# Head pairs of an RWKV-7 unit in lock-step: small matmuls as unbroken runs, low-rank weights of 128 rows

## The chip, the cores and the metric

The kernel runs on one core of a Trainium2 chip. Five engines work at the same time, each through its own instructions in order: TensorE (PE, matmuls; PEld is its weight loading), VectorE (DVE), ScalarE (ACT), GpSimd (POOL) and SyncE (SP, which here only issues DMAs). The metric is the time of one execution in microseconds; less is better.

## The reference

Two layers of a decoder trunk over 512 tokens of width 1024, in float32. Each layer is a half-step SwiGLU FFN, a mixer and another half-step FFN. The mixer of layer 0 is RWKV-7 time mixing, that of layer 1 a convolution module. The change is in the time mixing:

```python
w = -jax.nn.softplus(-(w0 + jnp.tanh(xw @ w1) @ w2)) - 0.5
a = jax.nn.sigmoid(a0 + (xa @ a1) @ a2)
...
def step(S, inp):
    r_t, w_t, k_t, v_t, a_t, b_t = inp
    sa = jnp.einsum('bhij,bhj->bhi', S, a_t)
    S = (S * w_t[:, :, None, :] + sa[..., None] * b_t[:, :, None, :]
         + v_t[..., None] * k_t[:, :, None, :])
    y_t = jnp.einsum('bhij,bhj->bhi', S, r_t)
    return S, y_t
```

There are 16 heads of size 64. w1, w2, a1 and a2 are low-rank: 1024 to 64 and 64 to 1024.

## The kernel before

Activations lie with the model dimension on the 128 partitions, in 8 blocks, and the 512 tokens along the free dimension. The large products (FFNs, projections) are made of float32 values split into two float32r parts, so each block product is three matmuls of a 128x128 weight against 256 or 512 columns ("wide" below). Weights come in tiles of eight 128x128 blocks (wr), which ACT rounds (wh) and DVE takes the rest of (wl).

The recurrence is done in chunks of 64 tokens. The work is cut into 8 units: unit u holds the head pairs 2q and 2q+1 (q = u mod 4) over one half of the tokens, the first half for units 0 to 3 and the second for units 4 to 7, so four chunks for each of its two pairs. Chunks 0 to 3 in the code are those of the first pair, 4 to 7 those of the second. `unit` has two parts. Part `a` makes the decays, the scaled keys (ka, bkc, bkh), the products G within each chunk, and inverts a triangular matrix block by block (DVE for 16x16 blocks, then matmuls X and D at two levels) into tt. Part `b` runs through the chunks. For each chunk and pair it makes z (PE, from the state in MV), copies it out of PSUM, multiplies by tt (PE), copies the result into UV, multiplies by bk (PE), and updates the state for the next chunk: the old state times the chunk's decay pc plus the product, one DVE instruction for each head. The last chunk's state goes to `carry`, which unit u + 4 starts from. Then y is made (PE), normalised over each head by a chain of small DVE instructions (gm, rq, ra, gr), and gated.

Matmuls differ in their form: 128 rows by 128 columns for the wide ones, 64 by 64 (G, X, D, z times tt, the second part of y), 128 by 64 (z from MV, the product with bk, the first part of y, tv), and 64 by 128 for the second low-rank factors: `step_w2` and the start of `unit` use the upper or lower 64 rows of blocks that hold w2 above a2. The two heads of a pair, h = 0 and 1, write different halves of the PSUM partitions. A small float32 product shows as two records in the trace.

The order of the program is set ahead of time. Every call on an engine goes to the class `Sched` (all of them then show as line 661), which lists the operations with their dependences and places them one by one, with a table of prices (`price`), a price for changing the form on PE (`SWITCH`), and a rule that looks for an operation of the same form first. Before the change nothing keeps the products of one group together. `hold` and `then` keep chains of small DVE instructions in one piece. Where the planner expects PE to stand still for long, it puts matmuls "warm" there, which read a constant and whose result nobody reads.

Of the kernel before, what the change touches and what calls it, by code (L numbers as in the profile page):

```python
# [18 lines left out]
P = 128  # L19
# [205 lines left out]
class Sched:  # L225
# [14 lines left out]
    SWITCH = 0.095  # L240
# [4 lines left out]
    def __init__(self, tc):  # L245
        self.tc = tc
        self.nc = tc.nc
        self.ops = []
        self.extra = []
        self.lead, self.chain, self.last = 0.0, 0, {}  # L250
        self.warmer, self.warm0 = None, 0
        self.hist = {}
        self.cap = {}
# [15 lines left out]
    @staticmethod  # L269
    def box(ap):  # L270
        dims = [tuple(d) for d in ap.ap]
        off = ap.offset
        name = ap.tensor.name
        if ap.space == bass.MemoryType.DRAM:
            return name, 0, 1, off, off + sum((n - 1) * s for s, n in dims) + 1
        ps, pn = dims[0]
        p0 = off // ps if ps else 0
        f0 = off - p0 * ps
        if ap.space == bass.MemoryType.PSUM:
            return name, p0, p0 + pn, 0, T  # L280
        return name, p0, p0 + pn, f0, f0 + sum((n - 1) * s for s, n in dims[1:]) + 1

# [4 lines left out]
    def add(self, engs, meth, args, kw):  # L287
# [57 lines left out]
        self.ops.append(op)  # L345

# [11 lines left out]
    def price(self, e, meth, args, kw, aps, n):  # L358
# [3 lines left out]
        if e == "tensor":  # L362
# [9 lines left out]
            return (0.053 if m > 32 else 0.027) if p0 else max(0.109, n * 1.69e-3)  # L372
# [33 lines left out]
    def order(self):  # L406
# [96 lines left out]
        while front < total:  # L503
            best = None
            for e, h in ready.items():
                if e == "bulk":
                    continue
                tmp, cand, n = [], None, 0
                while h and n < LOOK:
# [40 lines left out]
            if e == "tensor" and not op.bulk and st <= clock[e] + 0.3:  # L550
# [121 lines left out]
class Net:  # L672
# [485 lines left out]
    def unit(self, p):  # L1158
# [141 lines left out]
        for b in LEVELS:  # L1300
            ps = self.psum(f"X{p}_{b}")
            for c in range(NC):
                sl = slice(c * CH, c * CH + CH)
                self.pair(ps[:, sl], G(gb, c, 0), src[:, sl], True, True)
            vec.tensor_tensor(c3(xs), c3(ps), bc(self.c(f"m{b}")), ALU.mult)
            ps = self.psum(f"D{p}_{b}")
            for c in range(NC):
# [3 lines left out]
                else:  # L1311
                    self.pair(ps[:, sl], xs[:, sl], tt[:, sl], True, True)
            if b < 32:
# [15 lines left out]
        ps = self.psum(f"tv{p}")  # L1329
        for c in range(NC):  # L1330
            sl = slice(c * CH, c * CH + CH)
            for h in range(2):
                mm(ps[oth[h], sl], v[:, sl], self.c(f"cen{h}"), start=True, stop=True)
        MV, UV = [S(f"mv{h}") for h in range(2)], [S(f"uv{h}") for h in range(2)]
# [21 lines left out]
        for ci in range(NC):  # L1356
            cc, i = divmod(ci, 2)
            c = i * (NC // 2) + cc
            last = cc == NC // 2 - 1
            sl = slice(c * CH, c * CH + CH)  # L1360
            nx = slice(c * CH + CH, c * CH + 2 * CH)
            pz = self.s.tile(self.ps, [P, T], F32, f"z{p}_{c}", "z", 2)
            z = self.s.tile(self.ms, [P, CH], F32, f"z{p}_{c}", "zs", 4)
            for h in range(2):
                mm(pz[own[h], 0:CH], KA(h, c)[:, :CH], MV[h][:, sl], start=True, stop=True)
            (nc.copier.copy if ZC else vec.tensor_copy)(z, pz[:, 0:CH])
            self.pair(pz[:, CH:2 * CH], tt[:, sl], z, True, True)
            for h, e in ((0, nc.copier if UC else nc.vector), (1, nc.copier if UC else nc.scalar)):
                o = own[h]
                (e.tensor_copy if h == 0 and not UC else e.copy)(UV[h][o, sl], pz[o, CH:2 * CH])  # L1370
            if last and hf:
                continue
            for h in range(2):
                mm(pz[own[h], 2 * CH:3 * CH], bk[c // 4][:, c % 4, h], UV[h][:, sl], start=True, stop=True)
            for h in range(2):
                o = own[h]
                d = self.carry[o, prs[i] * CH:prs[i] * CH + CH] if last else MV[h][o, nx]
                vec.scalar_tensor_tensor(d, MV[h][o, sl], pc[o, c:c + 1],
                                         pz[o, 2 * CH:3 * CH], ALU.mult, ALU.add)
        py = self.psum(f"y{p}")  # L1380
        self.s.after("tensor", UV[1][own[1], YW * CH:YW * CH + CH], 2)
        for c in range(NC):
            sl = slice(c * CH, c * CH + CH)
            for h in range(2):
                mm(py[own[h], sl], MV[h][:, sl], KA(h, c)[:, CH:], start=c == 0, stop=False,
                   skip_group_check=True)
        for c in range(NC):
            sl = slice(c * CH, c * CH + CH)
            for h in range(2):
                o = own[h]  # L1390
                mm(py[o, sl], UV[h][o, sl], G(gb, c, 1)[o], start=False, stop=c == NC - 1,
                   skip_group_check=True)

# [229 lines left out]
class Weights:  # L1623


    def __init__(self, i):
# [10 lines left out]
        self.w2 = blocks(np.concatenate([i["rwkv_w2"][0], i["rwkv_a2"][0]], 0))  # L1637
# [3 lines left out]
    def of(self, kind, *a):  # L1641
# [16 lines left out]
        if kind in ("a", "b"):  # L1658
            q = a[0] % (NB // 2)
            s = self.w2 if kind == "a" else self.g2  # L1660
# [80 lines left out]
```

## Time and profile before

| | |
|---|---|
| median of 3 runs | 2221.14 us (2214.95 to 2223.2) |
| time of the profiled execution | 2214.0 us |
| its span, first to last instruction | 2212.2 us |
| PE busy | 2166.0 us, 98% |
| DVE busy | 1308.6 us, 59% |
| ACT busy | 862.1 us, 39% |
| POOL busy | 514.1 us, 23% |
| mean granted PE clock | 0.995 of full speed |

An engine's busy time is the union of its instructions' spans. The shares are means over stages with different work. The time mixing with its projections lies between about 400 and 960 us of the span.

### The profile page before, as it was taken

What the parts mean: (1) busy time and instruction counts of PE and PEld (TensorE: products, weight loads), DVE (VectorE), ACT (ScalarE), POOL (GpSimd) and SP (SyncE); (2) the same over time, 40 slices, a digit from 0 to 9 for tenths busy, and PEclk for the clock granted to TensorE, in tenths of its full rate; (3) what the DMA queues carried; (4) which work ended last, traced back from release to release, by engine and by line L of the source; (5) the groups of instructions that cost most, each with busy time, mean ns of one, the idle gap of its engine ahead of it and who ended that gap; (6) DMA issues with size and microseconds to landing.
All of it is one profiled execution on the core that took longest, in us unless ns stands there. A gap on an engine that the chain in (4) does not pass through costs nothing.

```text
span 2212.2 us, 38080 instructions
## 1 busy us (share of the span) xinstructions
PE 2166.0 (98%) x15523; PEld 1869.9 (85%) x15523; DVE 1308.6 (59%) x2201; ACT 862.1 (39%) x1374; POOL 514.1 (23%) x488
## 2 busy tenths in 40 slices
PE   9999999899999999999999999999999999999998
PEld 7888889577777888899999888888877799988898
DVE  5333347878788779576443434334469987744454
ACT  4222235555643454454322322122331266532343
POOL 2110113462443143022011112112220142311100
PEclk9999999999999999999999999999999999999999
DMA  4333337123224243356423333333335645543465
GB/s 160 96 95 105 96 105 208 55 78 88 71 71 136 68 122 108 88 179 188 137 93 96 95 94 97 95 95 95 95 108 148 179 137 182 182 132 93 129 189 154
DMA packets 120464, 262.21 MB, mean 119 GB/s; under 512 B 47072, under 2 KB 59744, under 8 KB 120288
## 3 DMA queue, kind: packets, MB, share of 16 engines
q1 hardware_dynamic: 86624, 254.52, 37.8%
q10 hardware_dynamic: 33664, 5.25, 1.3%
q8 instruction: 122, 2.00, 0.4%
q14 instruction: 54, 0.44, 0.1%
HBM read 250.19 MB, written 9.54 MB: 117 GB/s over the span
## 4 chain that ended last, share of the span: by engine, by line
PE 68%; DVE 6%; issue 1%; POOL 1%; ACT 1%; DMA 0%; ACTq 0%; DVEq 0%; POOLq 0%
PE f1d L661 6%; PE f3d L661 6%; PE f3g L661 6%; PE f3u L661 6%; PE f2g L661 6%; PE f2u L661 6%; PE f2d L661 6%; PE f1g L661 5%; PE f1u L661 5%; PE co L661 2%; PE wo L661 2%; PE cg L661 2%; PE ca L661 2%; PE dwx L661 2%; DVE wl L661 1%; PE v L661 1%
## 5 line engine op out<-in xcount | busy, mean ns | idle before, releaser
L661 ACT CAST wh<-wr 128x1024 fp32r<-128x1024 f32 (+1 forms) x448 | 467.4, 1045 | 1017.3 <-issue 376.2
L661 DVE TENSOR_TENSOR wl<-wr,wh 128x1024 fp32r<-128x1024 f32 (+1 forms) x448 | 554.9, 1240 | 263.0 <-ACT wh L661 249.3
L661 POOL TENSOR_TENSOR f0ss<-f0ss,n0rs 128x512 f32<-128x512 f32 x22 | 39.4, 1791 | 255.5 <-ACT f0ss L661 255.5
L661 POOL TENSOR_TENSOR f2ss<-f2ss,n2rs 128x512 f32<-128x512 f32 x22 | 38.8, 1762 | 250.3 <-ACT f2ss L661 250.3
L661 POOL TENSOR_TENSOR f3ss<-f3ss,n3rs 128x256 f32<-128x256 f32 (+1 forms) x33 | 49.6, 1505 | 193.0 <-ACT f3ss L661 193.0
L661 POOL TENSOR_TENSOR f1ss<-f1ss,n1rs 128x256 f32<-128x256 f32 (+1 forms) x33 | 45.2, 1372 | 211.3 <-ACT f1ss L661 190.1
L661 PE MATMUL f3g<-f_h,wh 128*128 128x256 f32 (+1 forms) x264 | 84.4, 320 | 0.0
L661 PE MATMUL f3g<-f_l,wh 128*128 128x256 f32 (+1 forms) x264 | 84.3, 319 | 0.0
L661 PE MATMUL f3u<-f_l,wh 128*128 128x256 f32 (+1 forms) x264 | 84.3, 319 | 0.0
L661 PE MATMUL f3g<-f_h,wl 128*128 128x256 f32 (+1 forms) x264 | 84.2, 319 | 0.0
L661 PE MATMUL f3u<-f_h,wl 128*128 128x256 f32 (+1 forms) x264 | 84.2, 319 | 0.0
L661 PE MATMUL f3u<-f_h,wh 128*128 128x256 f32 (+1 forms) x264 | 84.2, 319 | 0.0
L661 PE MATMUL f0g<-f_2h,wh 128*128 128x512 f32 x176 | 69.6, 396 | 2.5 <-ACT wh L661 2.5
L661 DVE SCALAR_TENSOR_TENSOR dwa<-ch,dw,dwa 128x256 f32<-128x256 f32 (+9 forms) x160 | 70.7, 486 | 0.9
L661 PE MATMUL f0g<-f_2l,wh 128*128 128x512 f32 x176 | 70.0, 398 | 0.8 <-DVE f_2l L661 0.7
L661 PE MATMUL f2u<-f_2h,wh 128*128 128x512 f32 x176 | 69.6, 395 | 0.0
L661 PE MATMUL f2g<-f_2l,wh 128*128 128x512 f32 x176 | 69.6, 395 | 0.0
L661 PE MATMUL f2u<-f_2l,wh 128*128 128x512 f32 x176 | 69.5, 395 | 0.0
L661 PE MATMUL f0u<-f_2h,wl 128*128 128x512 f32 x176 | 69.5, 395 | 0.0
L661 PE MATMUL f2g<-f_2h,wl 128*128 128x512 f32 x176 | 69.4, 395 | 0.0
L661 PE MATMUL f0u<-f_2h,wh 128*128 128x512 f32 x176 | 69.4, 395 | 0.0
L661 PE MATMUL f0g<-f_2h,wl 128*128 128x512 f32 x176 | 69.4, 394 | 0.0
(1505 smaller groups left out, 6806.0 us busy)
## 6 DMA issues: line engine op xcount, KB each, us to landing
wr<-wst SPq DMA_DIRECT2D x444, 512.0 KB, 3.6
hr<-hd SPq DMA_DIRECT2D x64, 65.0 KB, 2.0
hr<-hd SPq DMA_DIRECT2D x64, 61.2 KB, 2.0
x<-xT SPq DMA_DIRECT2D x8, 256.0 KB, 6.4
xspill<-x SPq DMA_DIRECT2D x8, 256.0 KB, 4.7
dl<-Gb ACTq DMA_DIRECT2D x16, 128.0 KB, 2.2
t<-dt ACTq DMA_DIRECT2D x8, 256.0 KB, 3.2
xr<-xspill SPq DMA_DIRECT2D x8, 256.0 KB, 5.3
```

The costliest lines, as they stand in the source:

```text
L661: self.tc.keep_in_program_order(getattr(eng, m)(*op.args, **op.kw))
```

## The change

Four things change.

- In part `b` the loop goes over 4 pairs of chunks, not over 8 chunks. One z tile holds both head pairs; z, the product with tt and the product with bk are each four products in a row; the copies and the state updates work on both pairs at once. The fused update (state times decay plus product) becomes two instructions: the state times the decay, written to the place of the next state before the product is there (on DVE or POOL, as the planner finds free), and an add of the product out of PSUM (DVE).
- `open` and `close` mark groups of products as a run. The first of a run takes over the dependences of all, and the rest follow it on PE with nothing between. The marked groups are G, X, D, tv, the three products of a step, and the two parts of y.
- The blocks of w2 and a2 get 64 rows of zeros each, and both are used with all 128 rows.
- `SWITCH` goes from 0.095 to 0.12, and the price of a small product on the second half of the partitions from 0.053 to 0.009. These are prices of the planner and act only through the order.

```diff
-    SWITCH = 0.095
+    SWITCH = 0.12
...
+    def open(self):
+
+        self.run = []
+
+    def close(self):
+
+        run, self.run = self.run, None
+        first, mine = run[0][0], {op.i for op, _ in run}
+        more = set().union(*(d for _, d in run)) - run[0][1] - mine
+        assert all(d < first.i for d in more)
+        for d in more:
+            self.ops[d].succ.append(first)
+        first.need += len(more)
+        for (a, _), (b, d) in zip(run, run[1:]):
+            a.then = b
+            if a.i not in d:
+                a.succ.append(b)
+                b.need += 1
+        for op, _ in run:
+            op.chain = -1
...
-            return (0.053 if m > 32 else 0.027) if p0 else max(0.109, n * 1.69e-3)
+            return (0.009 if m > 32 else 0.027) if p0 else max(0.109, n * 1.69e-3)
...
+                nx = hold.get(e)
+                if nx and nx.chain < 0:
+                    st = max(clock[e], nx.ready, free(nx, e))
+                    if best is None or (st, nx.i) < best[:2]:
+                        best = (st, nx.i, e)
+                    continue
...
-        self.mmw(ps, wh[:CH], wl[:CH], self.lth[:CH], self.ltl[:CH], True, True)
+        self.mmw(ps, wh, wl, self.lth, self.ltl, True, True)
...
-            self.mmw(pa[:, cols(i)], wh[CH:], wl[CH:], lth[CH:, hc], ltl[CH:, hc], True, True)
+            self.mmw(pa[:, cols(i)], wh, wl, lth[:, hc], ltl[:, hc], True, True)
...
-        for ci in range(NC):
-            cc, i = divmod(ci, 2)
-            c = i * (NC // 2) + cc
...
+        for cc in range(NC // 2):
             last = cc == NC // 2 - 1
...
+            self.s.open()
+            for i, (c, sl) in enumerate(at):
+                for h in range(2):
+                    mm(part(0, i, own[h]), KA(h, c)[:, :CH], MV[h][:, sl], start=True, stop=True)
+            self.s.close()
+            nc.copier.copy(z, pz[:, 0:n2])
+            if not (last and hf):
+
+                for h in range(2):
+                    o = own[h]
+                    d = (self.carry[o, prs[0] * CH:prs[0] * CH + n2].rearrange("p (i x) -> p i x", i=2)
+                         if last else two(MV[h], cc + 1)[o])
+                    nc.both.tensor_tensor(
+                        d, two(MV[h], cc)[o], pc[o, cc::NC // 2].unsqueeze(2).broadcast_to([CH, 2, CH]), ALU.mult)
...
-                vec.scalar_tensor_tensor(d, MV[h][o, sl], pc[o, c:c + 1],
-                                         pz[o, 2 * CH:3 * CH], ALU.mult, ALU.add)
+                d = (self.carry[o, prs[0] * CH:prs[0] * CH + n2].rearrange("p (i x) -> p i x", i=2)
+                     if last else two(MV[h], cc + 1)[o])
+                vec.tensor_tensor(d, both(2, o), d, ALU.add)
         py = self.psum(f"y{p}")
-        self.s.after("tensor", UV[1][own[1], YW * CH:YW * CH + CH], 2)
...
-        self.w2 = blocks(np.concatenate([i["rwkv_w2"][0], i["rwkv_a2"][0]], 0))
+        z = np.zeros((P - CH, D), np.float32)
+        self.w2 = blocks(np.concatenate([i["rwkv_w2"][0], z], 0))
+        self.a2 = blocks(np.concatenate([z, i["rwkv_a2"][0]], 0))
```

How this moves the instructions shows in the order on each engine. First PE, in the first step of unit 0 (z0_0 and z0_4 are the z tiles of the two pairs before, z0_0 holds both now; v2 is a value projection, tk11 a transposition, both wide). Before:

```order
L661 MATMUL v2_0_973<-mx3_0_6h_913,wh100_930 128x256
L661 MATMUL v2_0_973<-mx3_0_6l_914,wh100_930 128x256
L661 MATMUL v2_0_973<-mx3_0_6h_913,wl100_931 128x256
L661 MATMUL z0_0_944<-mv1_0_938,ka10_0_730 64x64
L661 MATMUL z0_4_946<-mv1_0_938,ka11_0_731 64x64
L661 MATMUL v2_0_973<-mx3_0_6h_913,wh100_930 128x256
L661 MATMUL v2_0_973<-mx3_0_6l_914,wh100_930 128x256
L661 MATMUL v2_0_973<-mx3_0_6h_913,wl100_931 128x256
L661 MATMUL z0_0_944<-z0_0_945,tt_0_748 64x64 x2
L661 MATMUL z0_4_946<-z0_4_947,tt_0_748 64x64 x2
```

The two products of head 0 (mv0) stand ten matmuls earlier, in a run of their own. And with the change:

```order
L691 MATMUL v2_0_965<-mx3_0_6h_913,wh100_930 128x256
L691 MATMUL z0_0_944<-mv0_0_937,ka00_0_728 64x64
L691 MATMUL z0_0_944<-mv1_0_938,ka10_0_730 64x64
L691 MATMUL z0_0_944<-mv0_0_937,ka01_0_729 64x64
L691 MATMUL z0_0_944<-mv1_0_938,ka11_0_731 64x64
L691 MATMUL v2_0_965<-mx3_0_6l_914,wh100_930 128x256
L691 MATMUL v2_0_965<-mx3_0_6h_913,wl100_931 128x256
L691 MATMUL tk11_1014<-cst_73,bkh1_1_787 128x128 x2
L691 MATMUL z0_0_944<-z0_0_945,tt_0_748 64x64 x4
```

All four products of z now stand together, head 0 and head 1 in turn, with one trip from wide to small in the place of two.

Second PE at the inversion of unit 1 (X1_16 is the product X at the first level, g1_0 and g1_1 are wide). Before:

```order
L661 MATMUL g1_0_893<-mx5_5l_880,wh96_867 128x512
L661 MATMUL X1_16_800<-t16_1_796,Gb0_1_789 64x64 x8
L661 MATMUL X1_16_800<-t16_1_796,Gb1_1_791 64x64
L661 MATMUL g1_0_893<-mx5_5h_879,wl96_868 128x512
L661 MATMUL g1_0_893<-mx5_6h_881,wh96_867 128x512
L661 MATMUL g1_0_893<-mx5_6l_882,wh96_867 128x512
L661 MATMUL g1_0_893<-mx5_6h_881,wl96_868 128x512
L661 MATMUL X1_16_800<-t16_1_796,Gb1_1_791 64x64 x7
L661 MATMUL g1_0_893<-mx5_7h_883,wh96_867 128x512
```

And with the change:

```order
L691 MATMUL g1_1_900<-mx5_3h_875,wl96_868 128x512
L691 MATMUL X1_16_800<-t16_1_796,Gb0_1_789 64x64 x8
L691 MATMUL X1_16_800<-t16_1_796,Gb1_1_791 64x64 x8
L691 MATMUL g1_1_900<-mx5_4h_877,wh97_895 128x512
L691 MATMUL g1_1_900<-mx5_4l_878,wh97_895 128x512
L691 MATMUL g1_1_900<-mx5_4h_877,wl97_896 128x512
L691 MATMUL g1_1_900<-mx5_5h_879,wh97_895 128x512
L691 MATMUL D1_16_801<-xs_1_799,tt_1_797 64x64 x16
```

The 16 products of X were in two pieces, cut in the middle of a pair; now they, and the 16 of D, are one piece each.

Third POOL at the end of the preparation of unit 3 (ka, bkc and bkh are its scaled keys, pc3 its decays, mv0_2 and mv1_2 the states of unit 2). Before:

```order
L661 TENSOR_TENSOR ka01_3_1079<-ru3_863,pt_3_1073 64x4x64
L661 TENSOR_TENSOR ka11_3_1081<-ru3_863,pt_3_1073 64x4x64
L661 COPY pc3_1082<-pt_3_1073 128x8
L661 TENSOR_TENSOR bkc0_3_1084<-k2_3_1086,ni_3_1074 64x4x64 x2
L661 TENSOR_TENSOR bkc1_3_1085<-k2_3_1086,ni_3_1074 64x4x64 x2
```

And with the change:

```order
L691 TENSOR_TENSOR ka01_3_1063<-ru3_863,pt_3_1057 64x4x64
L691 TENSOR_TENSOR ka11_3_1065<-ru3_863,pt_3_1057 64x4x64
L691 COPY pc3_1066<-pt_3_1057 128x8
L691 TENSOR_TENSOR mv0_2_1094<-mv0_2_1094,pc2_985 64x2x64
L691 TENSOR_TENSOR mv1_2_1095<-mv1_2_1095,pc2_985 64x2x64
L691 TENSOR_TENSOR bkc0_3_1068<-k2_3_1070,ni_3_1058 64x4x64 x2
L691 TENSOR_TENSOR bkc1_3_1069<-k2_3_1070,ni_3_1058 64x4x64 x2
```

Two decay products of unit 2 now stand in POOL's queue behind the ka of unit 3. There were none on POOL before.

## Rows read from the trace of the kernel before

**Rows 1.** The page: busy time, share of the span and instructions of each engine.

```profile
PE 2166.0 (98%) x15523; PEld 1869.9 (85%) x15523; DVE 1308.6 (59%) x2201; ACT 862.1 (39%) x1374; POOL 514.1 (23%) x488
```

**Rows 2.** Busy time by stretch: stretch, its length, engines, granted clock, DMA.

```profile
600.00:650.00 50.00, 44.77 (x468) 36.77 (x468) 42.31 (x113) 23.17 (x50) 17.49 (x26) 0.93 0.27 71
650.00:700.00 50.00, 45.84 (x605) 39.83 (x601) 44.80 (x125) 22.41 (x51) 16.45 (x24) 1.00 0.39 111
700.00:750.00 50.00, 45.93 (x639) 37.93 (x637) 39.80 (x110) 18.91 (x46) 16.05 (x22) 0.93 0.27 77
...
sum 460.00, PE 437.34 PEld 376.53 DVE 359.50 ACT 226.94 POOL 145.01; mean PE 48.59 PEld 41.84 DVE 39.94 ACT 25.22 POOL 16.11
```

The first three columns after the length are PE, PEld and DVE, then ACT and POOL; the sum is over 500 to 960 us.

**Rows 3.** PE in order of time around one X: start, length, operation, records.

```profile
521.92 0.40 PE L661 MATMUL k<-mx_3h,wh 128*128 128x512 f32 x1
522.15 0.40 PE L661 MATMUL k<-mx_3l,wh 128*128 128x512 f32 x1
522.48 1.15 PE L661 MATMUL X<-t,Gb 64*64 64x64 f32 x32
523.56 0.50 PE L661 MATMUL k<-mx_3h,wl 128*128 128x512 f32 x1
```

**Rows 4.** PE in order of time, first step of unit 0.

```profile
575.01 0.28 PE L661 MATMUL v<-mx_6h,wl 128*128 128x256 f32 x1
575.23 0.45 PE L661 MATMUL z<-mv,ka 128*64 128x64 f32 x4
575.60 0.39 PE L661 MATMUL v<-mx_6h,wh 128*128 128x256 f32 x1
575.83 0.29 PE L661 MATMUL v<-mx_6l,wh 128*128 128x256 f32 x1
575.96 0.28 PE L661 MATMUL v<-mx_6h,wl 128*128 128x256 f32 x1
576.16 0.45 PE L661 MATMUL z<-z,tt 64*64 64x64 f32 x8
576.54 0.55 PE L661 MATMUL tk<-cst,bkh 128*128 128x128 f32 x3
```

**Rows 5.** PE in order of time, one small form behind another.

```profile
681.55 0.45 PE L661 MATMUL z<-uv,bk 128*64 128x64 f32 x8
681.93 0.79 PE L661 MATMUL y<-Gb,uv 64*64 64x64 f32 x18
682.65 0.39 PE L661 MATMUL v<-mx_4h,wl 128*128 128x256 f32 x1
```

**Rows 6.** Waits of PE, 500 to 960 us: total, times, longest.

```profile
PE z L661 <- DVE mv L661: 5.0, 12, 1.5
PE gb L661 <- ACT gr L661: 3.9, 3, 2.2
```

**Rows 7.** PE in order of time, low-rank products of unit 2.

```profile
577.88 0.38 PE L661 MATMUL a<-lth,wh 64*128 64x256 f32 x1
578.10 0.28 PE L661 MATMUL a<-ltl,wh 64*128 64x256 f32 x1
```

**Rows 8.** Groups of the recurrence on DVE: count, busy us and mean ns, idle before.

```profile
L661 DVE SCALAR_TENSOR_TENSOR mv<-mv,pc,z 64x64 f32<-64x64 f32 x96 | 26.8, 279 | 12.2 <-PE z L661 4.1 <-ACT uv L661 3.4 <-ACT z L661 1.8
L661 DVE COPY uv<-z 64x64 f32<-64x64 f32 x34 | 7.5, 222 | 5.4 <-PE z L661 4.9
L661 DVE COPY z<-z 128x64 f32<-128x64 f32 x22 | 4.7, 220 | 4.0 <-PE z L661 3.6
L661 DVE SCALAR_TENSOR_TENSOR carry<-mv,pc,z 64x64 f32<-64x64 f32 x16 | 4.5, 279 | 2.7 <-PE z L661 2.3
```

**Rows 9.** All engines in order of time at one wait of PE.

```profile
671.28 1.26 POOL L661 TENSOR_TENSOR k24l<-k,k24h 128x512 fp32r<-128x512 f32 x1 [3.96 <-issue]
671.41 1.21 DVE L661 TENSOR_TENSOR lt<-lt,tm 64x60 f32<-64x60 f32 x1
...
673.37 0.28 PE L661 MATMUL z<-mv,ka 128*64 128x64 f32 x2 [1.50 <-DVE mv L661]
```

More of the change, by code (lines that the diff above doesn't have):

```diff
@@ L252, in __init__ @@
         self.hist = {}
+        self.run = None
         self.cap = {}
@@ L345, in add @@
         self.ops.append(op)
+        if self.run is not None and engs[0] == "tensor":
+            self.run.append((op, deps))
     @staticmethod
@@ L549, in order @@
             op = ops[i]
-            if e == "tensor" and not op.bulk and st <= clock[e] + 0.3:
+            if e == "tensor" and not op.bulk and st <= clock[e] + 0.3 and hold.get(e) is not op:
                 rest = (win + 1) * self.TICK + self.PH - st
@@ L1301, in unit @@
             ps = self.psum(f"X{p}_{b}")
+            self.s.open()
             for c in range(NC):
@@ L1329, in unit @@
         ps = self.psum(f"tv{p}")
+        self.s.open()
         for c in range(NC):
@@ L1354, in unit @@
         self.gate[p] = d
-        for ci in range(NC):
-            cc, i = divmod(ci, 2)
-            c = i * (NC // 2) + cc
+        two = lambda t, c: t.rearrange("p (i x) -> p i x", i=2)[:, :, c * CH:c * CH + CH]
+        n2 = 2 * CH
+        for cc in range(NC // 2):
             last = cc == NC // 2 - 1
[L1360 to L1363, printed above, removed]
-            for h in range(2):
[L1365 to L1370, printed above, removed]
+            at = [(c, slice(c * CH, c * CH + CH)) for c in (cc, cc + NC // 2)]
+            pz = self.s.tile(self.ps, [P, T], F32, f"z{p}_{cc}", "z", 2)
+            z = self.s.tile(self.ms, [P, n2], F32, f"z{p}_{cc}", "zs", 3)
+            part = lambda k, i, o=slice(0, P): pz[o, k * n2 + i * CH:k * n2 + i * CH + CH]
+            both = lambda k, o: pz[o, k * n2:k * n2 + n2].rearrange("p (i x) -> p i x", i=2)
+            self.s.open()
+            for i, (c, sl) in enumerate(at):
+                for h in range(2):
+                    mm(part(0, i, own[h]), KA(h, c)[:, :CH], MV[h][:, sl], start=True, stop=True)
+            self.s.close()
+            nc.copier.copy(z, pz[:, 0:n2])
[6 more added lines that the diff above has]
+                        d, two(MV[h], cc)[o], pc[o, cc::NC // 2].unsqueeze(2).broadcast_to([CH, 2, CH]), ALU.mult)
+            self.s.open()
+            for i, (c, sl) in enumerate(at):
+                self.pair(part(1, i), tt[:, sl], z[:, i * CH:i * CH + CH], True, True)
+            self.s.close()
+            for h in range(2):
+                nc.copier.copy(two(UV[h], cc)[own[h]], both(1, own[h]))
@@ L1371, in unit @@
             if last and hf:
                 continue
-            for h in range(2):
-                mm(pz[own[h], 2 * CH:3 * CH], bk[c // 4][:, c % 4, h], UV[h][:, sl], start=True, stop=True)
+            self.s.open()
+            for i, (c, sl) in enumerate(at):
+                for h in range(2):
+                    mm(part(2, i, own[h]), bk[c // 4][:, c % 4, h], UV[h][:, sl], start=True, stop=True)
+            self.s.close()
             for h in range(2):
                 o = own[h]
-                d = self.carry[o, prs[i] * CH:prs[i] * CH + CH] if last else MV[h][o, nx]
-                vec.scalar_tensor_tensor(d, MV[h][o, sl], pc[o, c:c + 1],
-                                         pz[o, 2 * CH:3 * CH], ALU.mult, ALU.add)
+                d = (self.carry[o, prs[0] * CH:prs[0] * CH + n2].rearrange("p (i x) -> p i x", i=2)
+                     if last else two(MV[h], cc + 1)[o])
+                vec.tensor_tensor(d, both(2, o), d, ALU.add)
@@ L1386, in unit @@
                    skip_group_check=True)
+        self.s.close()
+        self.s.open()
         for c in range(NC):
@@ L1659, in of @@
             q = a[0] % (NB // 2)
-            s = self.w2 if kind == "a" else self.g2
+            s = self.a2 if kind == "a" else self.g2
             return [s[2 * q], s[2 * q + 1]]
```

6 lines of the change are left out of this document (added).

## The prediction

> **What bounds the kernel now.** Read first the share of each engine: TensorE (PE) is busy for 98% of the span [rows 1], so time is won only where PE does less or waits less. The table by stretches then shows the stage of the recurrence, about 500 to 960 us; the changed lines work only there. PE is still its fullest engine: 437.34 of 460 us, against 359.50 us on VectorE (DVE). The stage has weak stretches, though: from 600 to 750 us PE is busy for 136.5 of 150 us, and in two of these three the granted clock is 0.93 [rows 2].
>
> A busy PE is not yet a PE that computes, so I read the order of time next, by starts. Matmuls of 128 rows by 128 columns ("wide") with 512 moving columns start 0.23 us apart. A run of 16 small products X (32 records, two to a product) begins 0.33 us after the last wide one, and the next wide one starts 1.08 us after the run's first record [rows 3]. With 256 moving columns, wide ones start 0.13 us apart in the middle of a stretch (575.83, 575.96) but the first two after a small run 0.23 us (575.60, 575.83) [rows 4]. So going in costs 0.10 us, the second wide one after coming out 0.10 us, and coming out itself the rest of the run. That rest follows from two runs of z: four products with both halves of the array side by side take 0.38 us (576.16 to 576.54), 16 products took 1.08 us; the difference, 0.70 us for 12, is 0.059 us a product, and 1.08 - 16 x 0.059 leaves 0.14. **A trip from wide to small and back costs 0.34 us, whatever it carries.** The run z at 575.23 has two products of one half only and takes 0.37 us [rows 4]: 0.23 without the exit, 0.115 each. **A product without its other half beside it costs 0.056 us more.** And a change from one small form to another: z x8 and y x18 take 1.10 us [rows 5]; 13 products at 0.059 and one exit are 0.91, so 0.19 us.
>
> Last the waits. In the stage PE waits 5.0 us, in 12 waits, for the state mv that DVE writes, and 3.9 us for gr, which the change doesn't touch [rows 6].
>
> **The change, part by part.**
>
> *Unbroken runs and low-rank weights of full height.* I counted both orders over all their PE rows. Trips from wide to anything smaller (the 64-row low-rank matmuls included) fall from 177 to 125: 52 x 0.34 = 17.7 us. Changes among the smaller forms fall from 40 to 14: 26 x 0.19 = 4.9 us. Products that stand without their other half fall from 172 of 1520 to none: 172 x 0.056 = 9.6 us. Together **-32 us of PE time**. Of the 172, 68 are G products of 128 columns, priced here by 64: at nothing they take 4 off, at double they add 4; a small change of form at the 0.10 of an entry takes 2 off. So 26 to 36.
>
> *The padding itself* costs nothing: the low-rank matmuls stream the same columns. The first two of 64 rows start 0.22 us apart [rows 7], as the first two wide ones after a change of form do [rows 4]. Nor does the stream of weights grow: w2 and a2 shared blocks of 128 rows, and each block was fetched once for w2 and once for a2, as many fetches as now.
>
> *The recurrence in lock-step.* A step of a unit, over its two head pairs, had two copies z, four copies uv and four fused updates; it now has one, two and two adds of twice the width, with two decay products ahead of them. DVE loses mv 26.8, carry 4.5, uv 7.5 and z 4.7 us, 43.5 in all [rows 8]. By the new order it gets 56 adds, 33 products, 12 and 7 copies. One of these costs at least the old 0.22 us of a copy and at most two old ones, 0.5; I take 0.29, near the lower end, as an op of 64 columns is mostly its start: 108 x 0.29 = 31 us (24 to 54). So DVE loses about 12 us, none of it on PE directly. Along a step's chain, four updates of 0.279 us in a row [rows 8] become two adds, 1.12 us becomes about 0.6, and the state is ready 0.5 us sooner, where the 12 waits average 0.42. Bounds: 0 (something else is late behind it) to 5.0 us; I take -2, since other rows wait for the same copies.
>
> *What the runs add.* A run starts only when the last of its inputs is there, and nothing can be put inside it. The order fills more: the matmuls "warm", which compute nothing, rise from 79 to 105, by 37 up to the second output projection and with 11 fewer after it. At the 0.23 us of a 512-column matmul [rows 3] the 37 are 8.6 us if PE pays them all, and 0 if each lies in a wait. I pay them in full, for the waits of [rows 6] are too few to hold them. The 11 stand where PE waits for a norm's chain or the program's end: 0. The two constants (SWITCH, the price of a second half) act through the order alone, which is counted.
>
> *A rule against the change.* The old update reads PSUM and one SBUF tensor. The new decay product reads two SBUF tensors, 33 times on DVE and 23 times on GpSimd (POOL). The row to weigh: a DVE op of 64x60 that begins at 671.41, just behind a POOL op of 1.26 us, takes 1.21 us and ends with it; the update queued behind it on DVE is late, and PE waits 1.50 us for mv [rows 9]. In the sum this stands at 0, as a product is issued while z and uv of its step are still to come, two visits to PE before its add; what it costs without that cover is rival 2. The Trainium skill ("SBUF — State Buffer", Who interferes with whom) says that a DVE instruction with two SBUF inputs contends with a GpSimd instruction that reads SBUF, and that the later one blocks until the first is done. The trace agrees in this row. By the rule all 56 products can block or be blocked, where none of the 112 updates could.
>
> Sum: -32 + 8.6 - 2 = **-25 us**. The profiled execution has a span of 2212.2 us and a time of 2214.0; the median of the runs shown, 2221.1, is 7 us above that. So I expect a span of 2187 us, and a median of **2196 us**. About 0.5%, 11 us, is what a measurement of this kernel can tell from no change.
>
> **Rivals.**
> 1. *DVE becomes the bound.* For: it is busy for 44.80 of 50 us from 650 to 700, and for 42.31 before [rows 2]; what it is full in, PE can't shorten. Then the gain is DVE's own 12 us, less half of the 8.6: -8 us, **2213 us**. Against: over the stage DVE would have 347 us of work in 435, 80%.
> 2. *The decay product comes late* (slower). 28 steps have products. POOL takes its own in order, behind the inputs of G and the 128x512 products. If each step's add waits as PE did for mv, 1.50 us [rows 9], with nothing to cover it, 28 x 1.50 = 42, and 42 - 32 + 8.6 = +19 us, **2240 us**. The change loses from 0.84 us a step, and by over 0.5% from 1.2. Against: several wide matmuls stand between the runs of a step, and POOL is busy for 145 of 460 us [rows 2].
> 3. *The fillers lie in waits, and the chain's waits go.* -32 - 5.0 and some of gr's 3.9: -40 us, **2181 us**. For: the chain is 0.5 us shorter where waits average 0.42. Against: PE then needs waits for the fillers that the trace before hardly shows.
> 4. *The clock.* 0.93 is a mean over the two levels, 2.4 and 1.2 GHz; a stretch at 0.93 loses 7% of 50 us, 3.5 us. Two have it now, and in the first of them stands PE's longest wait for gr, 2.2 us [rows 2, 6]. If runs that wait for their last input made such waits common, seven more stretches would cost 24 us: **2220 us**. Against: the 37 fillers of 512 columns.
>
> **How the numbers follow.** Forecast, -17 to -36 us (2185 to 2204): 0.56. Rival 1: 0.18. Rival 2: 0.08. Rival 3: 0.12. Rival 4: 0.06. The range leaves out rival 2, rival 4 and the edges of 1 and 3: 2178 to 2216. Faster by over 0.5%: 0.56 + 0.12 + a fifth of rival 1, 0.72. Slower by over 0.5%: 0.08. Within: 0.20.
>
> **What would show it.** Right: X and D come only with 32 records and z with 8; small products take the same time in a run, with fewer trips; the second output projection begins about 25 us sooner, and what follows lasts as long as before; PE waits for mv less than 3 us. Wrong: waits of z and y for mv, uv or ka above 15 us in all (rival 2, or runs that wait for their last input); DVE over 46 of 50 us in several stretches (rival 1); more stretches at a clock of 0.93 or less (rival 4); a time changed outside this stage, for which no term stands here.

## The result and the profile after

The changed kernel takes 2201.65 us (median of 4 runs, 2198.88 to 2202.39), the kernel before, beside it, 2218.05: a ratio of 0.9927, 95% interval 0.9908 to 0.9946. That is 16.4 us, 0.7%, faster; 2196 us, and a range from 2178 to 2216, were forecast. The profiled execution has a span of 2200.0 us (before 2212.2), 13 us over the 2187 that the sum gave.

Where the 12 us of span came from is read from the first start of a tile in either trace. The third feed-forward network (f2g) begins at 1231.9 us instead of 1259.4: the time mixing gained 27.5 us, where the sum had 25. (The second network is interleaved with its end; the second output projection already begins 27.3 us sooner, at 926.7 instead of 954.0, so the gain is made before 960 us, where it was forecast.) From f2g to the end it takes 968.2 us instead of 952.9, 15.3 us more. They are lost in the convolution: from its first product ca to f3g, the first of the network behind it, 189.0 us instead of 172.7; 1 us comes back elsewhere. The change touches no line of the convolution.

The page, as [rows 1]:

```profile
PE 2142.0 (97%) x15549; PEld 1860.0 (85%) x15549; DVE 1303.5 (59%) x2139; ACT 852.6 (39%) x1315; POOL 537.6 (24%) x513
```

Busy time by stretch, with the columns of [rows 2]:

```profile
600.00:650.00 50.00, 45.33 (x535) 38.77 (x531) 45.80 (x99) 26.55 (x50) 27.86 (x39) 0.97 0.29 79
650.00:700.00 50.00, 43.68 (x665) 37.37 (x665) 46.98 (x119) 19.34 (x39) 26.39 (x33) 1.00 0.36 89
...
800.00:850.00 50.00, 46.36 (x495) 42.90 (x494) 48.70 (x121) 22.29 (x39) 24.84 (x27) 1.00 0.46 124
...
sum 460.00, PE 435.65 PEld 386.37 DVE 372.52 ACT 233.11 POOL 175.06; mean PE 48.41 PEld 42.93 DVE 41.39 ACT 25.90 POOL 19.45
```

PE is busy for about as long in these 460 us as before, but part of this is work that came later before. DVE is fuller, 45.8 to 48.7 of 50 us in these stretches, where 44.80 was the most shown before [rows 2].

Waits of PE, 500 to 960 us, as [rows 6]: total, times, longest.

```profile
PE v L691 <- DVE wl L691: 5.5, 7, 1.5
PE v L691 <- ACT wh L691: 3.7, 4, 1.4
PE X L691 <- DVE ti L691: 3.0, 1, 3.0
PE f1g L691 <- DVE wl L691: 2.3, 3, 0.9
...
PE z L691 <- DVE mv L691: 1.3, 4, 0.5
```

The kernel before, the waits of the same product v:

```profile
PE v L661 <- DVE wl L661: 1.7, 3, 1.0
PE v L661 <- ACT wh L661: 0.3, 1, 0.3
```

The waits for mv fell from 5.0 to 1.3 us, under the forecast 3, and those for gr, which the forecast left alone, from 3.9 to 0.3. In their place PE waits for the two parts of the weights of its wide products, wh from ACT and wl from DVE: over all products 15.0 us, where it was 4.0 before.

The groups of the recurrence on DVE, as [rows 8]: count, busy us and mean ns, idle before.

```profile
L691 DVE TENSOR_TENSOR mv<-z,mv 64x128 f32<-64x128 f32 x48 | 13.8, 288 | 12.9 <-PE z L691 10.0 <-ACT uv L691 0.9 <-ACT gr L691 0.7
L691 DVE TENSOR_TENSOR mv<-mv,pc 64x128 f32<-64x128 f32 x27 | 8.6, 320 | 0.5
L691 DVE COPY uv<-z 64x128 f32<-64x128 f32 x12 | 3.4, 287 | 2.0 <-PE z L691 1.9
L691 DVE TENSOR_TENSOR carry<-mv,pc 64x128 f32<-64x128 f32 x6 | 3.2, 525 | 0.1
L691 DVE TENSOR_TENSOR carry<-z,carry 64x128 f32<-64x128 f32 x8 | 2.3, 286 | 0.7 <-PE z L691 0.6
L691 DVE COPY z<-z 128x128 f32<-128x128 f32 x7 | 2.0, 286 | 0.1
```

They come to 33.3 us for the 43.5 removed, near the forecast 31.

**The convolution.** PE in order of time where it lost: start, length, operation, records, and in brackets the idle time before and its releaser.

```profile
1732.23 1.17 PE L691 MATMUL lnv<-cst,lsq 128*128 128x1 f32 x10
1733.33 7.97 PE L691 MATMUL dwx<-hr,dg 128*32 128x256 f32 x140
1745.70 4.93 PE L691 MATMUL dwx<-hr,dg 128*32 128x256 f32 x40 [4.40 <-DMA hr<-hd]
1750.56 2.39 PE L691 MATMUL lnv<-cst,lsq 128*128 128x1 f32 x20
...
1756.15 1.19 PE L691 MATMUL ln0bc<-cst,ly 128*128 128x128 f32 x4 [1.46 <-DVE ly L691]
...
1761.18 0.80 PE L691 MATMUL co<-cs_0h,wh 128*128 128x256 f32 x2 [3.41 <-ACT cs_0h L691]
```

The norm of the first half (lnv, then lm and ly on DVE, ln0bc, cs, co) needs 16 products lnv, two records each. Six go early; ten stand behind 90 products dwx of the second half, the last 20 of which wait 4.40 us for a DMA. The wide products ca and cg are used up by 1732, about as long after the first ca as before (130 us, 128 before), and now the dwx too by 1750, so little is left to fill the holes. The clock falls too (columns of [rows 2]):

```profile
1730.00:1750.00 20.00, 15.25 (x205) 9.47 (x204) 13.49 (x26) 4.02 (x10) 5.85 (x7) 0.84 0.36 98
1750.00:1770.00 20.00, 14.45 (x81) 12.06 (x76) 14.39 (x30) 11.76 (x27) 10.40 (x13) 0.64 0.00 0
```

### The profile page after: what moved, and what is told of

The parts are those of the page before. It is cut to its first block, busy times and chain, and to the rows that moved or that the text cites. A ratio compares the mean times of both kernels' runs of the same rounds, so it can differ in the third digit from the quotient of the medians.

```text
span 2200.0 us, 37992 instructions
## 1 busy us (share of the span) xinstructions
PE 2142.0 (97%) x15549; PEld 1860.0 (85%) x15549; DVE 1303.5 (59%) x2139; ACT 852.6 (39%) x1315; POOL 537.6 (24%) x513
## 4 chain that ended last, share of the span: by engine, by line
PE 67%; DVE 8%; issue 2%; DMA 1%; POOL 1%; ACT 1%; SPq 0%; ACTq 0%; DVEq 0%; POOLq 0%
PE f1d L691 6%; PE f3d L691 6%; PE f3g L691 6%; PE f3u L691 6%; PE f2u L691 6%; PE f2g L691 6%; PE f2d L691 6%; PE f1g L691 5%; PE f1u L691 5%; PE co L691 2%; PE wo L691 2%; DVE wl L691 2%; PE ca L691 2%; PE dwx L691 1%; PE cg L691 1%
## 5 line engine op out<-in xcount | busy, mean ns | idle before, releaser
L691 POOL TENSOR_TENSOR f2ss<-f2ss,n2rs 128x512 f32<-128x512 f32 x22 | 38.8, 1765 | 250.8 <-ACT f2ss L691 250.8
L691 DVE SCALAR_TENSOR_TENSOR dwa<-ch,dw,dwa 128x256 f32<-128x256 f32 (+8 forms) x160 | 72.4, 495 | 1.1
L691 PE MATMUL f2u<-f_2h,wl 128*128 128x512 f32 x176 | 69.7, 396 | 0.0
L691 PE MATMUL f0u<-f_2l,wh 128*128 128x512 f32 x176 | 69.6, 396 | 0.0
```

Source lines behind the costliest of these rows:

```text
L691: self.tc.keep_in_program_order(getattr(eng, m)(*op.args, **op.kw))
```

## The experiments

In all but two of the runs everything from the norm ahead of the third network on (called the rest) is put, on every engine, in the order that the kernel before has there, fillers included, so that the time mixing can be compared by itself; run 2 has the changed kernel's order there, run 8 the planner's own. The edit that does this, `LATER` being the table of the order:

```diff
                     tmp.append(k)
+                    if i >= self.cut and (not turnof[e] or turnof[e][-1] != i):
+                        continue
...
+            if e == "tensor" and i >= self.cut:
+                for _ in range(fill[i]):
...
+                    out.append(None)
```

Spans and starts are of the profiled executions; "rest" is the span less the start of f2g; the ratio is to the kernel before, timed beside each.

| run | median us | ratio, 95% interval | f2g begins | rest |
|---|---|---|---|---|
| before (profile) | 2218.05 | | 1259.4 | 952.9 |
| changed | 2201.65 | 0.9927, 0.9908 to 0.9946 | 1231.9 | 968.2 |
| 1 changed, old rest | 2189.5 | 0.9875, 0.9851 to 0.9900 | 1230.3 | 955.0 |
| 2 before, new rest | 2229.7 | 1.0051, 1.0035 to 1.0068 | 1261.9 | 965.8 |
| 3 constants alone | 2207.7 | 0.9959, 0.9942 to 0.9976 | 1254.3 | 953.7 |
| 4 no lock-step | 2200.3 | 0.9922, 0.9896 to 0.9947 | 1241.0 | 954.1 |
| 5 no runs | 2204.5 | 0.9931, 0.9915 to 0.9947 | 1248.2 | 954.4 |
| 6 no padding | 2190.9 | 0.9867, 0.9849 to 0.9885 | 1233.1 | 955.9 |
| 7 no fillers | 2191.3 | 0.9866, 0.9848 to 0.9883 | 1238.7 | 951.7 |
| 8 old SWITCH in the convolution | 2187.1 | 0.9850, 0.9834 to 0.9865 | 1232.4 | 952.9 |
| 9 trips added | 2198.3 | 0.9917, 0.9897 to 0.9936 | 1242.3 | 953.2 |
| 10 halves apart | 2196.0 | 0.9908, 0.9888 to 0.9928 | 1239.9 | 953.8 |
| 11 decay on VectorE | 2187.9 | 0.9868, 0.9845 to 0.9890 | 1236.2 | 956.6 |
| 12 old constants | 2195.6 | 0.9900, 0.9873 to 0.9926 | 1240.8 | 954.2 |

Since the rest takes 952 to 957 us in every run with an order like the old one, the start of f2g tells what the time mixing took in the profiled execution. One order gives it within 2.5 us: that of the changed kernel was profiled three times (itself, runs 1 and 8: 1230.3 to 1232.4) and that of before twice (1259.4, 1261.9). Differences of that size tell nothing, and where start and ratio say different things, this is noted.

**Runs 1 and 2: the two halves exchanged.** Edit: the table above, taken from the other kernel.

> The changed kernel, but from the norm ahead of the third feed-forward network on, every instruction stands on its engine in the order (and every filler at the place) that the kernel before has there; up to there nothing is changed. Theory A (the time mixing gained 27.5 us as the sum said, and the convolution gave back 15 to 17 us only because its instructions were put in another order): the third network still begins at about 1232 us, the first co matmul comes about 27 us sooner than before, near 1749 us, PE no longer waits 4.4 us for hr, and the span is 2182 to 2188 us, 24 to 30 under before. Theory B (the convolution lost time for another reason, for example because the weights or the data in DRAM reach it at another phase): the convolution again lasts 15 us longer, the span stays at 2197 to 2203 us.

> The kernel before, with the order of the changed kernel from the norm ahead of the third feed-forward network on; up to there the kernel before. Theory A (the order of the convolution alone costs 15 to 17 us): the third network begins at 1259 us as before, the convolution lasts 12 to 17 us longer than before, and the span is 2224 to 2230 us, 12 to 18 over before, with the same wait of PE for hr. Theory B (another reason, tied to what runs ahead): within 5 us of before, 2208 to 2217 us.

Theory A held both ways: the rest goes from 968.2 to 955.0 us with the old order, and from 952.9 to 965.8 with the new one under the old time mixing, so 13 of the 15.3 us go with the order. In run 1 all 16 lnv stand together, ahead of the last dwx; PE in order of time:

```profile
1734.70 3.63 PE L876 MATMUL dwx<-hr,dg 128*32 128x256 f32 x50
1738.26 3.73 PE L876 MATMUL lnv<-cst,lsq 128*128 128x1 f32 x32
1741.86 4.12 PE L943 MATMUL warm<-idr 128*128 128x512 f32 x10
1745.82 0.60 PE L876 MATMUL ln0bc<-cst,ly 128*128 128x128 f32 x4
1746.18 1.64 PE L943 MATMUL warm<-idr 128*128 128x512 f32 x6
1747.74 2.35 PE L876 MATMUL dwx<-hr,dg 128*32 128x256 f32 x34
1750.02 0.50 PE L876 MATMUL co<-cs_0h,wh 128*128 128x256 f32 x2
```

co begins at 1750.0 instead of 1761.2, fillers cover the chain of the norm, and the 34 records left of dwx cover the way from ln0bc to co. The clock of the same stretches:

```profile
1730.00:1750.00 20.00, 19.96 (x208) 14.39 (x206) 19.50 (x49) 8.14 (x18) 5.75 (x6) 0.91 0.33 88
1750.00:1770.00 20.00, 19.49 (x155) 18.31 (x155) 17.28 (x28) 16.11 (x35) 13.90 (x13) 1.00 0.34 105
```

**Run 8: is it SWITCH that put it so?**

```diff
     def step_conv(self):
+        self.s.cut = len(self.s.ops)
...
+            if front >= self.cut:
+                self.SWITCH = 0.095
```

> The changed kernel with the constant SWITCH put back to 0.095 from the convolution on (0.12 up to there); nothing replayed. The convolution's order comes out anew: of the 16 variance products lnv of the first half 10 stand before and 6 behind a run of 51 small convolution products (in the changed kernel 6 before and 10 behind 90), and 20 small products are left for behind the norm's transposes. Theory G (the loss lies in the first half's norm, whose last products are queued behind that run, one of them waiting for its data by DMA): the norm is done some 6 to 10 us sooner, co begins about 150 us after ca instead of 159, span 2184 to 2193 us. Rival B (the convolution is slower for a reason outside its order): span 2197 us or more.

Theory G: co begins 145.5 us after ca (159.0 in the changed kernel, 146.9 before; about 150 was expected), the rest takes 952.9 us, and the median is the lowest of the study, 1.5% under the kernel before. That 0.095 gives a good order of the convolution in general does not follow: another start of the stage gives another order.

**Runs 3 and 12: the constants.** Run 3 puts them into the kernel before, run 12 takes them out of the changed one:

```diff
-    SWITCH = 0.12
+    SWITCH = 0.095
...
-            return (0.009 if m > 32 else 0.027) if p0 else max(0.109, n * 1.69e-3)
+            return (0.053 if m > 32 else 0.027) if p0 else max(0.109, n * 1.69e-3)
```

> The kernel before with the two constants of the change (SWITCH 0.12, price of a second half 0.009) and nothing else of it, and with the order of before from the norm ahead of the third network on. Theory A (the gain of the time mixing comes from unbroken runs; the constants only reorder): its order has 180 trips for 177, 54 changes among small forms for 40, 158 unpaired products for 172 and 14 more fillers up to the second output projection, which at the prices of the prediction is 1.0 + 2.7 - 0.8 = +2.9 us and up to +3.2 for the fillers: the third network begins 0 to 6 us later than before, span 2212 to 2218 us. Rival C (the constants give much of the gain, by an order with fewer waits): the third network begins 10 us sooner or more, span under 2202 us.

> The changed kernel with both constants of before (SWITCH 0.095, price of a second half 0.053), lock-step, runs and padding kept, and the order of before from the norm ahead of the third network on. Its order has 126 trips, 18 changes among small forms, no unpaired product and 76 fillers up to the second output projection (125, 14, 0, 91). Theory A (what counts is PE's own work in the order): +0.34 + 0.76 us, and at most 3.5 less for 15 fillers: the third network begins between 1228 and 1232 us, span 2182 to 2187 us. Rival C (the constants give a part of the gain by an order in which PE waits less, as they gave 5.1 us alone): the third network begins 5 us later than in the first run or more, at 1235 us or later, with more waits of PE there.

Both theories missed run 3: f2g begins 5.1 us sooner, neither the 0 to 6 later of A nor the 10 of C. Run 12 is C's: without the constants f2g begins 10.5 us later, though the order has as many trips, within one. By the ratios the constants are worth 9 us in run 3 (0.41%) and 5.5 us between runs 1 and 12. A count of trips and products does not tell an order's time: waits and clock count too.

**Runs 4, 5 and 6: the parts.** Run 4 has the recurrence of before, in the words of the diff's removed lines, with all else of the change. Runs 5 and 6:

```diff
     def close(self):
-        run, self.run = self.run, None
+        self.run = None
+        return
```

```diff
-        self.mmw(ps, wh, wl, self.lth, self.ltl, True, True)
+        self.mmw(ps, wh[:CH], wl[:CH], self.lth[:CH], self.ltl[:CH], True, True)
...
-            self.mmw(pa[:, cols(i)], wh, wl, lth[:, hc], ltl[:, hc], True, True)
+            self.mmw(pa[:, cols(i)], wh[CH:], wl[CH:], lth[CH:, hc], ltl[CH:, hc], True, True)
```

> The changed kernel with the recurrence of before (one chunk at a time, fused updates; no runs there but for tv and y), the runs of G, X, D kept, the weights padded, and the order of before from the norm ahead of the third network on. Its order has 165 trips, 40 changes among small forms, 44 unpaired products and 87 fillers up to the second output projection (before 177, 40, 172, 54; after 125, 14, 0, 91). Theory A (PE's own time by the three prices): against before 12 x 0.34 + 128 x 0.056 = -11.3 us, and +7.6 for 33 fillers if PE pays them: the third network begins 4 to 11 us sooner than before, span 2201 to 2208 us. Rival D (the runs of X, D and G, which stand in both, are the gain, and the lock-step little): within 5 us of the first run of this set, 2182 to 2192 us.

> The changed kernel without unbroken runs (lock-step, padded weights and constants kept; each small product may again stand alone), with the order of before from the norm ahead of the third network on. Its order has 159 trips, 33 changes among small forms, 208 unpaired products and 65 fillers up to the second output projection (with the runs 125, 14, 0, 91). Theory A (the three prices): against the first run of this study 34 x 0.34 + 19 x 0.19 + 208 x 0.056 = +26.8 us, less up to 6.0 for the fillers: the third network begins 20 to 27 us later than there, at 1250 to 1257 us, span 2205 to 2213 us. Rival D (the lock-step itself, its fewer and wider VectorE instructions and its shorter chain, makes the gain): within 8 us of the first run, the third network before 1239 us.

> The changed kernel with the low-rank weights of 64 rows as before, with the order of before from the norm ahead of the third network on. Its order has 132 trips (125 with padding), 30 changes among the smaller forms (14) and 97 fillers (91) up to the second output projection. Theory A (padding is worth the changes of form it removes): 7 x 0.34 + 16 x 0.19 = +5.4 us, up to 6.8 with the fillers: the third network begins at about 1236 us, span 2190 to 2193 us. Rival E (a change of the number of rows alone costs PE nothing): within 2 us of the first run of this study, 2183 to 2188 us.

Run 4: f2g at 1241.0, 18.4 us sooner than before, more than A's 4 to 11, and 10.7 later than run 1, more than D's 5, so neither theory held; the constants, at 5.1 us in run 3, are in it. Run 5: 17.9 us later than run 1, 2 short of A's 20 to 27, far over D's 8. Without runs, the lock-step, the padding and the constants together keep 11 of 29 us (by the ratios 15 of 28); what the lock-step keeps alone was not measured. Run 6: 2.8 us later, span 3.6 us over run 1, where A had 5.4. But in both, 2.2 to 2.4 us of this are there at 440 us (the first r product starts at 442.0 and 442.2, in run 1 at 439.8), ahead of the recurrence and of the products that are padded, and the time of run 6 is that of run 1 within their spread. So the padding shows no worth of its own here, as rival E had it.

**Runs 9 and 10: two prices measured by themselves.** Every engine keeps the order of run 1. In run 9 two wide matmuls move into the middle of each of 40 runs; in run 10 the halves inside a run X no longer alternate. On the list of PE's instructions, `a` to `b` being a run:

```diff
+    two = pe[b:b + 2]
+    pe[b:b + 2] = []
+    pe[(a + b) // 2:(a + b) // 2] = two
```

```diff
+    pe[a:b] = pe[a:b:2] + pe[a + 1:b:2]
```

> The first run of this study (the changed kernel with the old order behind the time mixing), every instruction and filler of every engine in the same order, but for one thing: at 40 of the unbroken runs (G, X, D, tv, y), the two wide matmuls that stood right behind the run now stand in its middle. 165 trips instead of 125, the same products and the same work. Theory A (a trip costs 0.34 us, whatever it carries): the third network begins 40 x 0.34 = 13.6 us later than in the first run, at about 1244 us, span about 2199 us; small to wide and wide to small grow by about 40 each in number and by 14 us less 40 ordinary starts of 0.12 us in time. Rival H (PE has slack enough in this stage, so that what a trip costs is taken from waits): less than 5 us.

> The first run of this study, every instruction and filler in the same order, but for one thing: in each of the 16 runs X the eight products of one half of the array come first and then the eight of the other half, instead of by turns. No trip and no product is added; 14 of the 16 products of a run lose their neighbour in the other half. Theory A (a product without its other half beside it costs 0.056 us more): 16 x 14 x 0.056 = 12.5 us, the time between starts in a run of 16 goes from about 0.93 to about 1.7 us, the third network begins at about 1243 us, span about 2198 us. Rival I (the pieces of a half follow each other as closely as by turns, and the cost was that of single products beside something else): less than 3 us.

Run 9, PE around one X in order of time, as [rows 3]:

```profile
519.39 0.40 PE L1076 MATMUL k<-mx_5l,wh 128*128 128x512 f32 x1
519.72 0.68 PE L1076 MATMUL X<-t,Gb 64*64 64x64 f32 x16
520.33 0.50 PE L1076 MATMUL k<-mx_5h,wl 128*128 128x512 f32 x1
520.67 0.40 PE L1076 MATMUL k<-mx_6h,wh 128*128 128x512 f32 x1
521.00 0.68 PE L1076 MATMUL X<-t,Gb 64*64 64x64 f32 x16
521.61 0.50 PE L1076 MATMUL k<-mx_6l,wh 128*128 128x512 f32 x1
```

From 519.72 to 521.61 are 1.89 us; less two wide starts of 0.23 and the 1.08 of an unbroken X [rows 3], 0.35 is left for the added trip. Over all 40, f2g begins 12.0 us later, 0.30 each, where 13.6 was expected (by the ratios the run is 9 us over run 1). Run 10, the same place:

```profile
519.35 1.90 PE L1075 MATMUL X<-t,Gb 64*64 64x64 f32 x32
521.17 0.50 PE L1075 MATMUL k<-mx_5h,wl 128*128 128x512 f32 x1
```

1.82 us instead of 1.08, so 0.74 / 14 = 0.053 for each product that lost its neighbour. f2g begins 9.6 us later (by the ratios 7); 12.5 was expected. The starts from one small product to the next grew by 12.0 us in all, and PE waited 4 us less.

**Run 7: are the fillers a cost?**

```diff
-            if e == "tensor" and self.warmer and ops[self.warm0].end is not None:
+            if e == "tensor" and not self.mix[0] <= i < self.mix[1] and self.warmer and ops[self.warm0].end is not None:
```

> The changed kernel without fillers from the start of the time mixing up to the second half of the second network's norm (17 instead of 91, the 30 around 395 to 440 us left out too), with the order of before from the norm ahead of the third network on; no other work is left out. Its order has 119 trips and 19 changes among small forms. Theory A (PE pays the fillers in full, as the sum had it): the third network begins 8 us sooner than in the first run of this study, at about 1222 us, if the clock stays. Rival F (the fillers hold the clock, and those that PE pays come back as stretches at half clock): more such stretches between 395 and 960 us than in the first run, and the third network begins at 1230 us or later.

`self.mix` holds the first and last operation of the stretch without fillers. Rival F, in the profiled execution: f2g begins 8.4 us later without them. The granted clock is lower; two stretches of this run (columns of [rows 2]):

```profile
390.00:450.00 60.00, 47.70 (x183) 34.95 (x183) 50.69 (x70) 31.33 (x59) 28.42 (x22) 0.83 0.13 41
...
800.00:850.00 50.00, 44.26 (x460) 40.49 (x455) 45.89 (x106) 20.79 (x36) 28.32 (x31) 0.90 0.38 100
```

The changed kernel has 0.97 and 1.00 there, run 1 0.94 and 1.00. Some 2 us of the 8.4 are there at 440 us already (the first r product starts at 441.8, in run 1 at 439.8), before the recurrence. From 440 us to f2g, counted as in the table of the next section, the 9.5 us that begin at a filler in run 1 are gone, but PE's waits are 8.3 us longer and its other intervals 9.7, which reads as if most of the fillers had lain in waits. The median is only 1.8 us over that of run 1, and the ratio no worse (0.9866 for 0.9875). So what holds beyond this one execution is that leaving the fillers out doesn't bring the 8 us of theory A; that it costs 8 is not shown.

**Run 11: the decay products on one engine.**

```diff
-                    nc.both.tensor_tensor(
+                    nc.vector.tensor_tensor(
```

> The changed kernel with all decay products on VectorE, none on GpSimd, with the order of before from the norm ahead of the third network on. Its order has 122 trips, 12 changes among small forms and 90 fillers up to the second output projection (125, 14, 91). Theory J (products on GpSimd beside VectorE's with two SBUF inputs draw these out, and the waits of PE for wl, 5.5 us for v and more for f1g and f1u in the first run, come from that): VectorE's lt and tm instructions are short again, PE waits for wl at least 3 us less, the third network begins 3 to 6 us sooner than in the first run, at 1224 to 1227 us. Rival K (VectorE is full where PE waits, 46.3 and 48.8 of 50 us from 650 to 700 and 800 to 850 us; 23 more products of 0.32 us make it later): the third network begins 2 to 6 us later, at 1232 to 1236 us.

J fell: the lt and tm instructions of DVE take 64.8 us in all (run 1 66.8), and PE's waits for wl are 10.3 us in all (10.0). K gives the start of f2g, 1236.2, but 3 us of the 5.9 are there at 440 us, ahead of the first such product; the profiled execution is the slowest of its four, and the medians of the two runs agree within 0.1%. Which engine has these products decides nothing that can be measured here.

## Why the prediction was right, and where it was not

The account of the time mixing comes from the starts of PE's records, from 440 us to the start of f2g. Each interval counts as what it leads from and to; what an interval of over 0.45 us has above 0.25 is put down as a wait.

```
us                         before  changed  run 3  run 12  run 5
small to small, same form   114.9     97.7  109.4   102.5  110.9
small to other small          9.0      2.9    9.8     3.6    8.1
small to wide                27.3     20.4   28.5    20.8   26.7
wide to small                39.6     30.1   41.7    30.4   38.5
from a filler                 2.1      9.4    5.1     7.4    3.3
wide to wide                604.3    605.2  605.5   608.1  603.2
waits                        22.0     26.0   14.3    27.7   17.4
```

- **-32 us for runs and full-height weights.** X and D come only with 32 records, as forecast, and X takes 1.08 us as before. The first four lines fall by 39.7, and wide to wide (low-rank products of either height among them) grows by 0.9 with 43 more intervals: 38.8 us less, over the 36 that the term allowed. What the clock cost is inside these numbers; at the rate of rival 4, the two stretches at 0.97 instead of 0.93 are some 4 us of them, an estimate. Two of the three prices were tested and hold: 0.35 and 0.30 us a trip for 0.34 (run 9), 0.053 for 0.056 (run 10). The third, 0.19 for a change among small forms, was not tested by itself; behind the 14 changes in the changed kernel the next start comes after 0.16 us on the mean, 0.13 above an ordinary small start of 0.03. Run 6 shows no gain from the full height.
- **+8.6 us for the fillers.** They take 7.3 us more of PE, as forecast. That they are a price was wrong: left out, waits grow by 8.3 us, the granted clock is lower, and nothing is gained (run 7). Rival 3 was nearer in this, but not in its other half, fewer waits.
- **-2 us for the lock-step's chain.** The wait for mv fell by 3.7 us, but waits as a whole rose by 4.0, outside the term's bounds of 0 to -5: what is late next is the split of the weights on DVE and ACT. DVE lost 5 us on the page, not 12: the new instructions took 33.3 us for 31, and its lt and tm instructions 6.1 us more than before (68.4 for 62.3). The Trainium skill ("SBUF — State Buffer", Who interferes with whom) says that a DVE instruction with two SBUF inputs contends with a GpSimd instruction that reads SBUF. By that, POOL's 23 decay products could be the cause. Taking them off POOL (run 11) took 2.1 us off lt and tm, of the 4.6 that run 1 has over before, so the trace bears that out for half of it at most.
- **The sum of 25 us for 27.5** is in part luck: PE's own term was 6.8 us too small, the fillers 1.3 us too dear, and the waits went 6.0 us the other way.
- **"The two constants act through the order alone, which is counted."** This step failed, though the time came out near the forecast with it. What was counted is trips, changes and products. With those nearly equal, the constants are worth 10.5 us (run 12 against run 1), and alone 5.1 us with more trips than before (run 3), where PE waits 7.7 us less. So of the 29.1 us of run 1, 18.6 are left without the constants: the 25 of the sum were met only with them. A part of the 10.5 can be read: from 550 to 850 us the granted clock of run 12 is 0.97, 0.90, 1.00, 0.97, 1.00 and 0.97 by stretches of 50 us, that of run 1 1.00, 0.93, 0.97 and then 1.00, some 4.5 us at the rate of rival 4 (an estimate). What in the orders makes the rest was not taken further.
- **"What follows lasts as long as before."** This step failed by 15.3 us, and is why the span came out at 2200 instead of 2187. The counting of the order stopped at the time mixing. Its own sign of being wrong, a time changed outside the stage, is what came. In the convolution SWITCH, or the other start of the stage, left the norm's last ten products behind 90 dwx, and no dwx behind them. Runs 1, 2 and 8 show that the order there is the cause, and run 8 that SWITCH brings it about from this start. That the position of lnv is what counts in that order is read from the trace, not tested by moving these ten products alone.
- **Rivals 1, 2 and 4** did not decide the time. Waits for mv are 1.3 us (2); no stretch from 500 to 960 us is under 0.97 (4). The sign of rival 1 did come, DVE at 47.0 and 48.7 of 50 us in two stretches and PE waiting for its wl, but the time mixing kept its gain.

That the median came within 6 us of the forecast is luck. The span was 13 us too long: 15.3 us that had no term, less 2.5 us more gain in the time mixing. Against that stands the step from span to median: the forecast added 9 us, because the profiled execution of before lay 7 us under its median, and in the changed kernel the median is 1.7 us over the span.

## What to carry to other kernels

Where one planner orders the whole program, a constant changed for one stage is a change to all of them: read the order of the other stages too, and look where the last filler work is used up before a chain that everything waits for. If the order of an untouched stage comes out worse, pin it; here that was worth 12 us beside the 16 of the change itself. Count trips between array forms and products without their other half, for they have stable prices, but check fillers by leaving them out before counting them as a cost: here leaving 74 out gained nothing.

## What the runs showed of the hardware

Small products of one half of the array, one behind another, take longer than products that alternate between halves: 16 took 1.82 us instead of 1.08 up to the next wide one, with nothing else changed (run 10). A trip costs about the same in the middle of a run of its own kind as between different ones: 0.35 us at one place, 0.30 each over 40 (run 9). In the convolution PE's records co start 0.21 us apart at the lower clock (1763.46, 1763.67; granted 0.50 from 1763 to 1766 us) and 0.12 apart at the higher (run 1: 1750.51, 1750.63; granted 1.00 from 1750 to 1752), so the stretch at 0.64 cost time beyond its waits.
